# A decoder trunk on one core: the opening transfers in the order of their use, and the mLSTM output factors worked out with tokens on partitions

## The chip, the cores and the metric

The kernel runs on one core of a Trainium2 chip. The metric is the time of one execution on the device in microseconds (us), the median of the runs shown. The engines are called by their names: TensorE (PE: matmuls and transposes), VectorE (DVE), ScalarE (ACT), GpSimd (POOL) and SyncE (SP), which issues most of the transfers.

## What is computed

A trunk of two layers on 512 tokens of width 1024, in float32. Each layer adds half a gated feed-forward block, a token mixer and another half block to the residual; the first layer's mixer is latent attention, the second's an mLSTM. The part of the mLSTM that the change touches is the end of a head: the quotient of `num` by a bounded `den`, a normalisation over the head's 128 values, a gain and a gate.

```python
def rmsnorm(x, g, eps=RMS_EPS):
    y = xf * lax.rsqrt(jnp.mean(xf * xf, axis=-1, keepdims=True) + eps)
    return (y * g.astype(F32)).astype(x.dtype)
...
        h = num / jnp.maximum(jnp.abs(den), jnp.exp(-m_t))[..., None]
...
    hid = mlstm_chunkwise(q, k, v, i_pre, log_f)
    hid = hid * lax.rsqrt(jnp.mean(hid * hid, axis=-1, keepdims=True) + RMS_EPS)
    hid = hid.reshape(B, S, V) * out_norm.astype(F32) * jax.nn.sigmoid(o.astype(F32))
    return hid.astype(h.dtype) @ w_o
...
        x = x + 0.5 * swiglu(rmsnorm(x, ffn_norm[layer, 0]), ffn_w_gate[layer, 0],
                             ffn_w_up[layer, 0], ffn_w_down[layer, 0])
```

With `a = max(|den|, exp(-m))` and `sq` the sum of the squares of `num`, the factor of a head and token is `(sq / 128 + EPS * a * a) ** -0.5`. The kernel works out this one number for every head and token and multiplies `num`, gain and gate by it.

## The kernel before

The activations lie transposed: channels on partitions, the 512 tokens along the free dimension. Every matmul is made of three, from a high and a low part of each operand (`whi`, `wlo` for weights; the first or second of a pair for activations). ScalarE makes the high part, VectorE the low one (`split_pieces`, L185 and L186). The program is written as one sequence, but a scheduler in the tile framework sets the order in which each engine takes its instructions; each engine then works strictly in its order, so an instruction that waits holds all those behind it.

*The opening.* `begin` runs warm-up matmuls of no use to the result, then loads the residual as eight tiles `x` (128x512, two to an arena tile) and the first two weight tiles in quarters (`raw`, 128x256). Quarter k of the first weight tile belongs to `x[k]`, quarter k of the second to `x[4 + k]`: six matmuls use such a pair. `norm_split` makes the parts of `x`. The constants `cst` hold the identity, masks and ones; `st` (L300) is the matmul of the squares `acc` with the ones, from which VectorE, GpSimd and ScalarE make the factor that the feed-forward block behind it waits for, and `bc` (L325) spreads it. SyncE issues the transfers in one queue.

*The mLSTM factors.* In `mlstm`, `mix` adds to one PSUM bank, `rows`, with a selecting weight `pick`: row h gets a head's `den`, row 32 + h its sum of squares, by six matmuls for a pair of heads. `factors` is a generator in three steps, called for heads 0 to 3 and again for 4 to 7. Its steps are put between other work with `defer(n, step)`: the step runs when the n-th weight tile from there is asked for.

- Step one: `a`, `sq` and `n` on 8 partitions x 512 tokens: |den| and a copy on ScalarE, three operations on VectorE. `em` is exp(-m), 8x512.
- Step two: four transposes into `ab` (tokens on partitions, 8 heads and 4 token tiles along the free dimension), the copy `fc` and the power -0.5 on GpSimd, `fp`.
- Step three: four transposes back into `fb`, split into `frows`. `gated` spreads a row over the partitions and multiplies.

In the first call the steps stand among the projections `qk` (the convolution's, `conv(3)`) and `v` (`values(1)`, four weight tiles of 24 matmuls); in the second among the output projections `y`. `columns` transposes other per-head rows into a bank `cb` once and copies them to `cols`.

Of the kernel before, what the change touches and what calls it, by code (L numbers as in the profile page):

```python
# [30 lines left out]
AF = mybir.ActivationFunctionType  # L31
ALU = mybir.AluOpType
AX = mybir.AxisListType

P = 128
# [3 lines left out]
NT = T // P  # L39
# [12 lines left out]
EPS = 1e-6  # L52
# [14 lines left out]
class Trunk:  # L67
# [68 lines left out]
    def load_pieces(self):  # L136

        name, pieces, pool, plus = self.loads[len(self.loaded)]

        ap = self.row(*name)  # L140
        raw = self.duo(pool, F32) if pool else self.wp.tile([P, W], F32, name="raw", tag="raw")
        self.loaded.append(raw)
        for a, b in pieces:
            queue = self.nc.gpsimd if plus and name[0] == "wgs" else self.nc.sync
            queue.dma_start(out=raw[:, a:b], in_=ap[:, a:b])
            yield
        if plus:
            self.nc.gpsimd.dma_start(out=raw, in_=self.row(*plus), accum_op=ALU.add)  # L148
# [185 lines left out]
    def begin(self, gcol):  # L334
        nc = self.nc
        self.used = 0
        self.later = []
        self.mhalf = self.const.tile([P, NT], F32, name="mhalf")
        nc.vector.memset(self.mhalf, -0.5)

        warm = self.small.tile([P, P], BF16, name="warm", tag="warm", bufs=1)
        nc.vector.memset(warm, 0.0)
        nc.scalar.copy(out=warm[:, 0:1], in_=warm[:, 1:2])
        idle = self.ps2.tile([P, T], F32, name="idle", tag="st")
        for i in range(WARM):
            nc.tensor.matmul(idle[:, 0:P], warm, warm, start=True, stop=True)
        self.par = self.const.tile([P, V_END], F32, name="par")
        nc.sync.dma_start(out=self.par, in_=self.t["vecs"])
        cst = self.const.tile([P, self.t["cst"].shape[1]], F32, name="cst")
        self.ident = cst[:, 0:P]  # L350
        self.mask = cst[:, P:2 * P]
        self.maskT = cst[:, 2 * P:3 * P]
        self.invf, self.sign, self.one = (cst[:, 3 * P + i:3 * P + i + 1] for i in range(3))
        self.sel = cst[:, 3 * P + 3:3 * P + 11]
        self.norm_begin(gcol)
        quarters = [(k * 256, k * 256 + 256) for k in range(4)]
        for i in range(2):
            self.loads[i] = self.loads[i][0], quarters, None, None
        for i in range(2):
            load, split = self.load_pieces(), self.split_pieces(quarters, False)  # L360
            for k in range(4):
                d = 4 * i + k
                nc.sync.dma_start(out=self.x[d], in_=self.t["xT"][d * P:(d + 1) * P, :])
                next(load)
                self.norm_split(d)
                next(split)
            list(load), list(split)
            if i == 0:
                nc.sync.dma_start(out=cst, in_=self.t["cst"])
        self.todo = list(range(ND))  # L370

    def constants(self):
# [614 lines left out]
    def mlstm(self, next_gain):  # L987
        nc = self.nc
        v, s = nc.vector, nc.scalar
        xg = self.xg  # L990
        g8 = slice(0, 8)
# [7 lines left out]
        def conv(i):  # L999

            b = self.bank("qk")
            self.project(self.weights("wqk", i), b)
            p, y = self.t512("p"), self.t512("conv")
            v.tensor_tensor(out=p, in0=b, in1=rb, op=ALU.mult)
            v.tensor_scalar(y, p, self.vec(V_CONVW + 3 * ND + i), self.vec(V_CONVB + i), ALU.mult, ALU.add)
            for j in range(1, 4):
                v.scalar_tensor_tensor(out=y[:, j:], in0=p[:, :T - j], scalar=self.vec(V_CONVW + (3 - j) * ND + i),
                                       in1=y[:, j:], op0=ALU.mult, op1=ALU.add)  # L1010
            s.activation(y, y, AF.Silu)
            pr = self.pair()
            if i < 4:
                qz = self.pair("qz")
                for z, e, o in ((qz[0], A, B), (qz[1], B, A)):
                    nc.gpsimd.memset(z[o].bitcast(F32), 0.0)
                    s.copy(out=z[e], in_=y[e])
                s.copy(out=pr[0][B], in_=y[A])
                s.copy(out=pr[1][A], in_=y[B])
                v.tensor_tensor(out=pr[0][A], in0=y[A], in1=qz[0][A].bitcast(F32), op=ALU.subtract)  # L1020
                v.tensor_tensor(out=pr[1][B], in0=y[B], in1=qz[1][B].bitcast(F32), op=ALU.subtract)
                pr = pr + qz
            else:
                self.halves([(pr[0][A], A), (pr[1][B], B)], [(pr[0][B], A), (pr[1][A], B)], y)
            qk[i] = pr
# [18 lines left out]
        tiles = lambda a: a.rearrange("p (a b) -> p a b", a=NT)  # L1044

        def turn(bank, c, src, row=0):

            n, m = src.shape
            nc.tensor.transpose(out=bank[0:m, c:c + n], in_=src, identity=self.ident[row:row + n, row:row + n])

        def small(name, n=32):
            return self.small.tile([P, n], F32, name=name, tag=name, bufs=1)
# [31 lines left out]
        rows, frows = self.pair()  # L1084
        em = self.small.tile([P, T], F32, name="em", tag="rb", bufs=2)
# [24 lines left out]
        values(0)  # L1110
        place = [(0, 0), (1, 0), (2, 0), (1, 384)]
        ws, sums, nums, ys, sg, sg_of, acc, which = {}, {}, {}, {}, {}, {}, {}, {}
        cols = small("cols", 80)

        def columns():

            cb = self.bank("cb")
            for i in range(NT):
                src = z[g8, i * P:(i + 1) * P]
                bt = self.t512("bt") if i < NT - 1 else None  # L1120
                for j in range(i, NT):
                    if j > i:
                        dst = bt[g8, (j - 1) * P:j * P]
                        v.tensor_scalar(dst, src, fl[g8, j * P - 1:j * P], None, ALU.add)
                        src = dst
                    which[i, j] = 8 * len(which)
                    turn(cb, which[i, j], src)
            s.copy(out=cols, in_=cb[:, 0:80])


        def spread(rows, h):
# [83 lines left out]
        def factors(half, squares):  # L1215

            for f in squares:
                f()
            a, n = self.t512("a"), self.t512("n")
            s.activation(a[g8], acc["rows"][g8], AF.Abs)  # L1220
            sq = self.t512("sq")
            s.copy(out=sq[g8], in_=acc["rows"][32:40])
            v.tensor_tensor(out=a[g8], in0=a[g8], in1=em[g8], op=ALU.max)
            v.scalar_tensor_tensor(out=n[g8], in0=a[g8], scalar=EPS, in1=a[g8], op0=ALU.mult, op1=ALU.mult)
            v.scalar_tensor_tensor(out=a[g8], in0=sq[g8], scalar=1.0 / P, in1=n[g8],
                                   op0=ALU.mult, op1=ALU.add)
            yield
            ab = self.bank("ab")
            for j in range(NT):
                turn(ab, 8 * j, a[g8, j * P:(j + 1) * P])  # L1230
            fc, fp = small("fc", 16), small("fp", 16)
            s.copy(out=tiles(fc), in_=tiles(ab[:, 0:32])[:, :, 4 * half:4 * half + 4])
            nc.gpsimd.tensor_tensor(out=fp, in0=fc, in1=self.mhalf[:, 0:1].broadcast_to([P, 16]), op=ALU.pow)
            yield
            fb = self.bank("fb")
            for j in range(NT):
                turn(fb, j * P, fp[:, 4 * j:4 * j + 4])
            self.split_to((frows[0:4], frows[32:36]), fb[0:4])
            yield
# [6 lines left out]
        def out(part, i, between=None):  # L1246
            self.mix_out("wo2", part, i, ys, between)
# [15 lines left out]
        for p in range(3):  # L1263
            a, b = 2 * p, 2 * p + 1
            conv(p + 5) if p < 2 else gate(5)
            gate(a + 2)
            pending = [mix(a), mix(b)]
            if p == 1:
                steps = factors(0, pending)
                for i in (1, 2, 4):  # L1270
                    self.defer(i, lambda: next(steps))
                conv(3)
                values(1)
                for i in range(4):
                    gated(i)
            if p == 0:
                gate(b + 2)
                for f in pending:
                    f()
            if p == 2:  # L1280
                out(0, 0)
            decay(a + 2)
            if p < 2:
                conv((2, 7)[p])
            else:
                for f in pending:
                    f()
            decay(b + 2)
# [203 lines left out]
```

## Time and profile before

| | |
|---|---|
| median of 3 runs | 1839.35 us (1837.66 to 1840.27) |
| the profiled execution | 1836.03 us, span 1834.3 us |
| TensorE busy | 1808.8 us, 99% of the span |
| VectorE, ScalarE, GpSimd busy | 80%, 51%, 10% |
| chain that ended last | TensorE 72%, issue 16%, VectorE 4%, transfers 3%, ScalarE 3%, GpSimd 1% |

A row of the timeline has the start and the duration in us, the engine, the line, the operation, output and inputs, and in brackets the idle time of that engine before it and what ended it. Matmuls overlap in the pipeline: the distance from one start to the next says what one costs, not its duration. The chain is followed back from the last instruction, and busy shares are averages over the whole span.

### The profile page before, as it was taken

Reading aid. Unit: us, or ns where it says so; the run is one execution under the profiler, and the core shown is the slowest. Engines: PE = TensorE matmul, PEld = TensorE weight load, DVE = VectorE, ACT = ScalarE, POOL = GpSimd, SP = SyncE. Lnnn points to the kernel's source line nnn. Section 1 sums busy time; section 2 is a strip of 40 time slices with the busy share of each in tenths; the row PEclk is TensorE's granted clock in tenths of the full one; section 3 lists DMA queues with packets and bytes.
Section 4 is the critical chain, followed back from the end, with each engine's and each line's share of the span. In section 5 each row is a group of like instructions: output and inputs, shape, how many; then the busy total and the mean of one; then the engine's idle time right before and its main releaser. Section 6 shows DMA issues by size and latency. Waiting matters only on the chain.

```text
span 1834.3 us, 30137 instructions
## 1 busy us (share of the span) xinstructions
PE 1808.8 (99%) x12258; PEld 1662.9 (91%) x12258; DVE 1458.8 (80%) x1934; ACT 938.6 (51%) x1350; POOL 181.3 (10%) x233
## 2 busy tenths in 40 slices
PE   9999999999999999999999999999999999999997
PEld 7999989978887999989989999997877779999897
DVE  7887898777767887877797879778878778788875
ACT  5544535567543444534544444455767544445344
POOL 1210001000001210000021000100010012100011
PEclk9999999999999999999999999999999999999999
DMA  8875376421126865466589356633212268753763
GB/s 273 241 221 152 120 189 150 138 75 64 47 94 196 234 190 149 137 184 152 196 217 265 105 162 190 167 106 112 81 63 70 74 186 249 202 151 117 188 150 104
DMA packets 80860, 282.45 MB, mean 154 GB/s; under 512 B 9105, under 2 KB 12305, under 8 KB 80721
## 3 DMA queue, kind: packets, MB, share of 16 engines
q1 hardware_dynamic: 52416, 179.06, 28.2%
q0 software_dynamic: 27728, 100.94, 25.4%
q8 instruction: 96, 1.57, 0.3%
q10 hardware_dynamic: 576, 0.52, 0.1%
q14 instruction: 44, 0.35, 0.1%
HBM read 270.01 MB, written 10.49 MB: 153 GB/s over the span
## 4 chain that ended last, share of the span: by engine, by line
PE 72%; issue 16%; DVE 4%; DMA 3%; ACT 3%; POOL 1%; SPq 0%; POOLq 0%; DVEq 0%; ACTq 0%
PE pz L481 4%; PE pw L479 4%; PE pz L479 4%; PE pw L480 4%; PE pz L480 4%; PE pw L481 4%; PE px L479 4%; PE px L480 4%; PE px L481 4%; PE y L217 3%; PE y L218 3%; PE y L219 3%; DMA sum<-in_wds 2%; PE py L479 2%; PE py L480 2%
## 5 line engine op out<-in xcount | busy, mean ns | idle before, releaser
L185 ACT CAST whi<-raw 128x1024 fp32r<-128x1024 f32 (+1 forms) x278 | 284.4, 1024 | 388.9 <-issue 120.7
L186 DVE TENSOR_TENSOR wlo<-raw,whi 128x1024 fp32r<-128x1024 f32 (+1 forms) x278 | 330.3, 1191 | 110.4 <-ACT whi L185 110.2
L185 ACT CAST whi<-sum 128x1024 fp32r<-128x1024 f32 x208 | 217.4, 1048 | 290.9 <-PE pz L480 72.9
L186 DVE TENSOR_TENSOR wlo<-sum,whi 128x1024 fp32r<-128x1024 f32 x208 | 253.1, 1221 | 67.4 <-ACT whi L185 67.2
L173 DVE TENSOR_TENSOR sum<-raw,sum 128x1024 f32<-128x1024 f32 x88 | 107.3, 1219 | 15.3 <-DMA raw<-in_wgs 14.6
L148 POOL DMA_DIRECT2D sum<-in_wgs x72 | 63.4, 880 | 290.1 <-DMA sum<-in_wgs 273.3
L481 PE MATMUL pz<-b5h,wlo 128*128 128x256 f32 x288 | 81.2, 282 | 0.6 <-DVE wlo L186 0.6
L479 PE MATMUL pz<-b5h,whi 128*128 128x256 f32 x288 | 81.3, 282 | 0.0
L479 PE MATMUL px<-b1h,whi 128*128 128x256 f32 x288 | 81.3, 282 | 0.0
L479 PE MATMUL pw<-b7h,whi 128*128 128x256 f32 x288 | 81.3, 282 | 0.0
L479 PE MATMUL px<-b2h,whi 128*128 128x256 f32 x288 | 81.3, 282 | 0.0
L480 PE MATMUL pw<-b4l,whi 128*128 128x256 f32 x288 | 81.3, 282 | 0.0
L480 PE MATMUL py<-b6l,whi 128*128 128x256 f32 x288 | 81.3, 282 | 0.0
L480 PE MATMUL px<-b1l,whi 128*128 128x256 f32 x288 | 81.3, 282 | 0.0
L479 PE MATMUL py<-b6h,whi 128*128 128x256 f32 x288 | 81.3, 282 | 0.0
L479 PE MATMUL pw<-b4h,whi 128*128 128x256 f32 x288 | 81.3, 282 | 0.0
L479 PE MATMUL pz<-b3h,whi 128*128 128x256 f32 x288 | 81.3, 282 | 0.0
L480 PE MATMUL pz<-b3l,whi 128*128 128x256 f32 x288 | 81.3, 282 | 0.0
L480 PE MATMUL pw<-b7l,whi 128*128 128x256 f32 x288 | 81.3, 282 | 0.0
L480 PE MATMUL px<-b2l,whi 128*128 128x256 f32 x288 | 81.3, 282 | 0.0
L480 PE MATMUL pz<-b5l,whi 128*128 128x256 f32 x288 | 81.3, 282 | 0.0
L481 PE MATMUL pz<-b3h,wlo 128*128 128x256 f32 x288 | 81.2, 282 | 0.0
(423 smaller groups left out, 6201.1 us busy)
## 6 DMA issues: line engine op xcount, KB each, us to landing
sum<-in_wgs POOLq DMA_DIRECT2D x144, 512.0 KB, 6.7
raw<-in_wgs SPq DMA_DIRECT2D x108, 512.0 KB, 5.6
sum<-in_wds POOLq DMA_DIRECT2D x48, 512.0 KB, 6.3
raw<-in_wds SPq DMA_DIRECT2D x48, 512.0 KB, 3.3
sum<-in_wds SPq DMA_DIRECT2D x32, 512.0 KB, 4.4
raw<-in_wgc SPq DMA_DIRECT2D x30, 512.0 KB, 3.6
raw<-in_wdn SPq DMA_DIRECT2D x24, 512.0 KB, 3.7
away<-x SPq DMA_DIRECT2D x16, 512.0 KB, 3.8
```

Source lines behind the costliest of these rows:

```text
L148: self.nc.gpsimd.dma_start(out=raw, in_=self.row(*plus), accum_op=ALU.add)
L173: self.nc.vector.tensor_tensor(out=t, in0=a, in1=b, op=ALU.add)
L185: self.nc.scalar.copy(out=hi[:, a:b], in_=raw[:, a:b])
L186: self.nc.vector.tensor_tensor(out=lo[:, a:b], in0=raw[:, a:b], in1=hi[:, a:b].bitcast(F32), op=ALU.subtract)
L217: mm(out, lhs[0], rhs[0], start=start, stop=False)
L218: mm(out, lhs[0], rhs[1], start=False, stop=False)
L219: mm(out, lhs[1], rhs[0], start=False, stop=stop)
L479: mm(out, wh, bh[:, b], start=first and e + k == 0, stop=False, skip_group_check=True)
L480: mm(out, wh, bl[:, b], start=False, stop=False, skip_group_check=True)
L481: mm(out, wl, bh[:, b], start=False, stop=last and e + k == 4, skip_group_check=True)
```

## The change

In the opening the transfers are written as eight pairs of an `x` and a weight quarter, with `cst` behind all of them; four memsets of one column make each `x` tile's first use an instruction of VectorE, behind which its transfers then stand. In the mLSTM, `em` is transposed with the other columns, step one of `factors` only copies the 40 rows to `both`, and the absolute value, the maximum and the sum are made behind the transposes, on 128 partitions x 16. In the first call the steps are deferred to the weight tiles 2, 3 and 5 instead of 1, 2 and 4.

```diff
-            queue = self.nc.gpsimd if plus and name[0] == "wgs" else self.nc.sync
...
+        for a in self.xt:
+            nc.vector.memset(a[:, 0:1], 0.0)
         for i in range(2):
             self.loads[i] = self.loads[i][0], quarters, None, None
-        for i in range(2):
-            load, split = self.load_pieces(), self.split_pieces(quarters, False)
-            for k in range(4):
-                d = 4 * i + k
+            load = self.load_pieces()
+            for d in range(4 * i, 4 * i + 4):
                 nc.sync.dma_start(out=self.x[d], in_=self.t["xT"][d * P:(d + 1) * P, :])
                 next(load)
-                self.norm_split(d)
+            list(load)
+        for i in range(2):
+            split = self.split_pieces(quarters, False)
+            for k in range(4):
+                self.norm_split(4 * i + k)
                 next(split)
-            list(load), list(split)
-            if i == 0:
-                nc.sync.dma_start(out=cst, in_=self.t["cst"])
+            list(split)
+        nc.sync.dma_start(out=cst, in_=self.t["cst"])
...
-        cols = small("cols", 80)
+        cols = small("cols", 112)
...
-            s.copy(out=cols, in_=cb[:, 0:80])
+            for j in range(NT):
+                turn(cb, 80 + 8 * j, em[g8, j * P:(j + 1) * P])
+            s.copy(out=cols, in_=cb[:, 0:112])
...
-            a, n = self.t512("a"), self.t512("n")
-            s.activation(a[g8], acc["rows"][g8], AF.Abs)
-            sq = self.t512("sq")
-            s.copy(out=sq[g8], in_=acc["rows"][32:40])
-            v.tensor_tensor(out=a[g8], in0=a[g8], in1=em[g8], op=ALU.max)
-            v.scalar_tensor_tensor(out=n[g8], in0=a[g8], scalar=EPS, in1=a[g8], op0=ALU.mult, op1=ALU.mult)
-            v.scalar_tensor_tensor(out=a[g8], in0=sq[g8], scalar=1.0 / P, in1=n[g8],
-                                   op0=ALU.mult, op1=ALU.add)
+            both = self.t512("both")
+            s.copy(out=both[0:40], in_=acc["rows"][0:40])
             yield
             ab = self.bank("ab")
             for j in range(NT):
-                turn(ab, 8 * j, a[g8, j * P:(j + 1) * P])
-            fc, fp = small("fc", 16), small("fp", 16)
-            s.copy(out=tiles(fc), in_=tiles(ab[:, 0:32])[:, :, 4 * half:4 * half + 4])
+                turn(ab, 40 * j, both[0:40, j * P:(j + 1) * P])
+            of = lambda t, c: tiles(t)[:, :, c + 4 * half:c + 4 * half + 4]
+            ab = ab[:, 0:160]
+            fa, fc, fp = small("fa", 16), small("fc", 16), small("fp", 16)
+            s.activation(tiles(fa), of(ab, 0), AF.Abs)
+            v.tensor_tensor(out=tiles(fa), in0=tiles(fa), in1=of(cols[:, 80:112], 0), op=ALU.max)
+            v.scalar_tensor_tensor(out=fa, in0=fa, scalar=EPS, in1=fa, op0=ALU.mult, op1=ALU.mult)
+            v.scalar_tensor_tensor(out=tiles(fc), in0=of(ab, 32), scalar=1.0 / P, in1=tiles(fa),
+                                   op0=ALU.mult, op1=ALU.add)
...
-                for i in (1, 2, 4):
+                for i in (2, 3, 5):
                     self.defer(i, lambda: next(steps))
```

The scheduler's order changes with it. On SyncE, at the start of the program, the rows before are these; `x_78` to `x_81` are the four arena tiles of the residual (two transfers each), `raw_129` and `raw_161` the first two weight tiles, `raw_194` the third.

```order
L348 DMA par_124<-in_vecs 128x111
L363 DMA x_78<-in_xT 128x512
L145 DMA raw_129<-in_wgc 128x256
L363 DMA x_78<-in_xT 128x512
L145 DMA raw_129<-in_wgc 128x256 x3
L369 DMA cst_126<-in_cst 128x395
L363 DMA x_79<-in_xT 128x512 x2
L145 DMA raw_161<-in_wgc 128x256 x4
L145 DMA raw_194<-in_wgc 128x1024
L363 DMA x_80<-in_xT 128x512 x2
L145 DMA raw_200<-in_wgc 128x1024
L363 DMA x_81<-in_xT 128x512 x2
```

Of the change, on SyncE at the same place (here `raw_133` and `raw_142` are the first two weight tiles, `raw_198` the third):

```order
L347 DMA par_124<-in_vecs 128x111
L363 DMA x_78<-in_xT 128x512
L144 DMA raw_133<-in_wgc 128x256
...
L363 DMA x_79<-in_xT 128x512
...
L363 DMA x_80<-in_xT 128x512
L144 DMA raw_142<-in_wgc 128x256
...
L363 DMA x_81<-in_xT 128x512
...
L372 DMA cst_126<-in_cst 128x395
L144 DMA raw_198<-in_wgc 128x1024
L144 DMA raw_204<-in_wgc 128x1024
```

Behind each `x` stands now one quarter of weights, and `cst` and the third weight tile have moved behind the last pair. On TensorE, in the first call of `factors`, the rows before are:

```order
L223 MATMUL rows<-pr,pick 128x512
L219 MATMUL qk<-pr,wlo 128x512
L217 MATMUL qk<-pr,whi 128x512
L218 MATMUL qk<-pr,whi 128x512
L219 MATMUL qk<-pr,wlo 128x512
L1049 MATMUL ab<-cst,a 128x8 x4
L217 MATMUL v<-whi,pr 128x512
```

Of the change, on TensorE at the same place, with the 24 `v` matmuls of the first weight tile cut:

```order
L217 MATMUL qk<-pr,whi 128x512
L218 MATMUL qk<-pr,wlo 128x512
L222 MATMUL rows<-pr,pick 128x512 x4
L216 MATMUL v<-whi,pr 128x512
...
L218 MATMUL v<-whi,pr 128x512
L1052 MATMUL ab<-cst,both 128x40 x4
L216 MATMUL v<-whi,pr 128x512
```

Four of the six `rows` matmuls have moved from among the `qk` matmuls to behind them, and `ab` from ahead of `v` to behind the first 24 of `v`; `fb` has moved by one weight tile as well. On VectorE, in the second call, before:

```order
L1310 TENSOR_TENSOR x<-y,x 128x512
L1223 TENSOR_TENSOR a<-a,em 8x512
L1224 SCALAR_TENSOR_TENSOR n<-a 8x512
L1310 TENSOR_TENSOR x<-y,x 128x512
L1225 SCALAR_TENSOR_TENSOR a<-sq,n 8x512
L186 TENSOR_TENSOR wlo<-raw,whi 128x1024
L1310 TENSOR_TENSOR x<-y,x 128x512 x2
```

Of the change, on VectorE at the same place:

```order
L1315 TENSOR_TENSOR x<-y,x 128x512 x2
L185 TENSOR_TENSOR wlo<-raw,whi 128x1024
L1234 TENSOR_TENSOR fa<-fa,cols 128x16
L1235 SCALAR_TENSOR_TENSOR fa<-fa 128x16
L1236 SCALAR_TENSOR_TENSOR fc<-ab,fa 128x16
L1315 TENSOR_TENSOR x<-y,x 128x512 x2
```

The three operations of 8x512 ahead of `wlo` are gone, and three of 128x16 stand behind it. On TensorE nothing moves in the second call.

## Rows read from the trace of the kernel before

**Rows 1.** Waits of TensorE, whole span: us in total, times, longest.

```profile
PE ab L1049 <- DVE a L1225: 3.9, 2, 2.4
```

**Rows 2.** Timeline of TensorE around `ab` in the first call.

```profile
1355.35 0.40 PE L219 MATMUL qk<-pr,wlo 128*128 128x512 f32 x1
1358.12 0.41 PE L1049 MATMUL ab<-cst,a 8*128 8x8 f32 x4 [2.37 <-DVE a L1225]
...
1359.03 0.60 PE L219 MATMUL v<-whi,pr 128*128 128x512 f32 x1
...
1362.67 0.39 PE L219 MATMUL v<-whi,pr 128*128 128x512 f32 x1
...
1371.09 0.39 PE L219 MATMUL v<-whi,pr 128*128 128x512 f32 x1
```

**Rows 3.** Windows behind both `ab`: busy us by engine, granted clock, DMA share, GB/s.

```profile
1359.00:1362.70 3.70, 3.70 (x11) 2.84 (x10) 2.81 (x4) 1.67 (x2) 3.70 (x1) 0.54 0.38 142
1440.80:1444.50 3.70, 3.70 (x11) 2.86 (x10) 0.14 (x1) 0.00 (x0) 2.44 (x1) 0.54 0.43 142
```

**Rows 4.** Timeline of all engines around `ab` in the second call.

```profile
1436.12 0.59 ACT L1220 ACTIVATE a<-rows 8x512 f32<-8x512 f32 x1 [2.30 <-PE rows L223]
...
1437.57 0.39 PE L219 MATMUL y<-pr,wlo 128*128 128x512 f32 x1
1437.77 1.04 ACT L185 CAST whi<-raw 128x1024 fp32r<-128x1024 f32 x1 [0.46 <-PE y L218]
...
1438.67 0.67 DVE L1225 SCALAR_TENSOR_TENSOR a<-sq,n 8x512 f32<-8x512 f32 x1
1439.27 1.21 DVE L186 TENSOR_TENSOR wlo<-raw,whi 128x1024 fp32r<-128x1024 f32 x1
...
1439.48 0.38 PE L1049 MATMUL ab<-cst,a 8*128 8x8 f32 x4 [1.52 <-DVE a L1225]
...
1440.21 3.03 POOL L1233 TENSOR_TENSOR fp<-fc,mhalf 128x16 f32<-128x16 f32 x1 [77.13 <-ACT fc L1232]
```

**Rows 5.** Timeline of TensorE behind `ab` in the second call.

```profile
1440.83 0.51 PE L218 MATMUL y<-pr,whi 128*128 128x512 f32 x1
...
1444.47 0.40 PE L218 MATMUL y<-pr,whi 128*128 128x512 f32 x1
```

**Rows 6.** Timeline of all engines in the opening (SPq issues transfers).

```profile
4.49 0.91 SPq L363 DMA_DIRECT2D x<-in_xT  x2
4.68 0.39 ACT L185 CAST whi<-raw 128x256 fp32r<-128x256 f32 x1
...
6.07 0.78 PE L217 MATMUL g<-pr,whi 128*128 128x512 f32 x1
...
7.44 0.39 PE L217 MATMUL u<-pr,whi 128*128 128x512 f32 x1
...
9.84 0.72 ACT L232 ACTIVATE pr<-x,par 128x512 fp32r<-128x512 f32 x1 [0.54 <-DMA x<-in_xT]
...
10.62 0.50 PE L217 MATMUL g<-pr,whi 128*128 128x512 f32 x1 [0.92 <-ACT pr L232]
...
14.44 0.50 PE L217 MATMUL g<-pr,whi 128*128 128x512 f32 x1 [0.43 <-ACT whi L185]
...
23.21 0.95 PE L300 MATMUL st<-cst,acc 128*128 128x1 f32 x8
```

**Rows 7.** Timeline of TensorE at `bc` in the opening.

```profile
27.55 0.47 PE L325 MATMUL bc<-diag,onesr 128*128 128x512 f32 x1 [0.24 <-DVE diag L321]
```

**Rows 8.** Instructions of tile zp: ns min/median/max, first and last start, forms.

```profile
L1078 DVE SCALAR_TENSOR_TENSOR zp<-zp,zu x5: 193/193/193, 1266.3 to 1267.2; 128x32 f32<-128x32 f32 x5
```

**Rows 9.** Timeline of GpSimd, the power in the first call.

```profile
1358.88 4.20 POOL L1233 TENSOR_TENSOR fp<-fc,mhalf 128x16 f32<-128x16 f32 x1 [25.45 <-ACT fc L1232]
```

**Rows 10.** Timeline of TensorE, transposes in `columns`.

```profile
1285.35 0.32 PE L1049 MATMUL cb<-cst,bt 8*128 8x8 f32 x3
```

**Rows 11.** The page's slices of 45.9 us: GB/s moved.

```profile
GB/s 273 241 221 152 120 189 150 138 75 64 47 94 196 234 190 149 137 184 152 196 217 265 105 162 190 167 106 112 81 63 70 74 186 249 202 151 117 188 150 104
```

More of the change, by code (lines that the diff above doesn't have):

```diff
@@ L138, in load_pieces @@
         name, pieces, pool, plus = self.loads[len(self.loaded)]
+        queue = self.nc.gpsimd if plus and name[0] == "wgs" else self.nc.sync
         ap = self.row(*name)
```

## The prediction

> **What bounds the kernel now.** TensorE: it is busy for nearly the whole span, so I first asked the view of its waits for the places where it stands still, and then read each place in the timeline. The reader is to see one name at the top of the waits: `ab` waiting for `a`, 3.9 us in two waits, the longest 2.4 [rows 1]. These are the two calls of `factors`. No other cause stands together like that at a place which the diff touches, except the opening.
>
> In the first call the last `qk` matmul starts at 1355.35 and `ab` at 1358.12 [rows 2]. A step between matmuls of 512 columns is (1371.09 - 1362.67) / 36 = 0.234 us there (36 steps lie between these two rows), so `ab` could have started at 1355.58 and the stop cost 2.54 us. Behind the stop there is a second price: from 1359.03 to 1362.67 nine steps take 3.64 us where nine at 0.234 take 2.10, and the granted clock of that stretch is 0.54 instead of 1.00, most of it at the lower of the two levels (1.2 instead of 2.4 GHz) [rows 2, 3]. That is 1.54 us more. The second call shows the same pair: from 1437.57 plus one step, 1437.80, to 1439.48 is 1.68 us of stop [rows 4], and from 1440.83 to 1444.47 nine steps take 3.64 us again at a granted clock of 0.54, 1.54 us more [rows 3, 5]. Together 2.54 + 1.54 + 1.68 + 1.54 = **7.30 us**.
>
> In the opening TensorE runs its warm-up matmuls until the first real one at 6.07, and reaches `st` at 23.21 with 61 matmuls between (the first of them the row at 6.07) [rows 6]. 61 steps of 0.234 end at 20.34, so 2.87 us are lost. The first three steps, 6.07 to 7.44, take 1.37 us instead of 0.70; the 0.67 us between follow the warm-ups whatever the transfers do, and I leave them. The rest, 2.20 us, are holes such as those before 10.62 and 14.44, with ScalarE named as the cause; ScalarE itself had waited for `x` (0.54 us before 9.84) [rows 6]. A hole of 0.24 us before `bc` comes on top [rows 7]. So at most 2.20 + 0.24 = **2.44 us** can be had in the opening.
>
> **The change, part by part.** *Factors, what is taken off the path.* The old chain from `rows` to `ab` is two copies on ScalarE, three VectorE operations on 8x512, 0.67 us for the last, with others queued among them: 1436.12 to 1439.48 in the second call [rows 4]. The new chain has one copy, `both`, in its place. It reads the same bank and as many columns as the old ones, 40 partitions instead of 8, so I take it at the 0.59 us of the nearest row; the bounds are nothing and 1.04 us (the row of `whi`, with twice the columns on 128 partitions) [rows 4]. In the second call `ab` stands where it stood. `both` would start at 1436.12 and end at 1436.71, at 1437.16 by the dear bound, and `ab` is due at 1437.80: no wait by either. In the first call the four last `rows` matmuls move behind all of `qk`, and `ab` behind the 24 matmuls of the first `v` chunk, 5.6 us later, which covers `both` by far. What `ab` waited for is thus gone in both calls, and with the stop the slow clock behind it: 7.30 us.
>
> *What is late next.* Behind `ab` come now `fa` on ScalarE, three VectorE operations on 128x16, the power on GpSimd, and `fb` on TensorE. Operations of 128x32 on VectorE take 0.193 us each, five in a row [rows 8]; 16 columns lie between nothing and that, and I take 0.22 us from one start to the next, 0.7 us for three. In the first call `fb` has moved too, two chunks of `v` (48 matmuls, 11.2 us) behind `ab`; the longest power here took 4.20 us [rows 9], so some 5 us are spare. In the second call `fb` stays 24 `y` matmuls behind `ab`: 1437.80 + 0.31 for `ab` + 24 x 0.234 = 1443.7. The chain there: `whi` holds ScalarE from 1437.77 for 1.04 us [rows 4], `fa` follows to 1438.95; VectorE has `wlo` (1.21 us [rows 4], from 1438.8 when `whi` is done) ahead of the three, so they end at about 1440.7; the power begins at 1440.75. With its 3.03 us [rows 4] it ends at 1443.8, a wait of 0.1 to 0.2 us; with the 4.20 us of the first call [rows 9] at 1444.95, a wait of 1.3 us. I take 0.2: in the second call VectorE has only `x<-y` during the power, as in the row of 3.03, where the call with 4.20 had `wlo` and three `conv` operations beside it.
>
> On this the Trainium skill has a rule ("SBUF — State Buffer", Who interferes with whom): a VectorE instruction with two SBUF inputs contends with a GpSimd instruction that reads SBUF, one with at most one SBUF input does not. `x<-y` has one input in PSUM, so by the rule the power keeps its short time and the wait is the 0.2 us of the sum; by the longer row alone it would be 1.3. The two rows, 3.03 and 4.20 us [rows 4, 9], agree with it.
>
> *What is added.* Four more transposes in `columns`: three of that kind took 0.32 us in all [rows 10], so four lie between 0.2 and 0.43 us; 0.25. They need `em`, made long before. `ab` moves 40 columns instead of 8, eight times in all: between nothing and 0.1 us; 0.1. The wider `cols` copy stands on ScalarE beside `og` matmuls of 5.6 us. So the factors give 7.30 - 0.25 - 0.1 - 0.2 = **6.75 us**; with both dear bounds 7.30 - 0.43 - 0.1 - 1.3, and 1.54 more if the wait at `fb` brings the slow clock, **3.9 us**.
>
> *Opening.* `x` now alternates with quarters of weights, and `cst` and the third weight tile come behind all of them. The third `x` had been issued at 4.49, behind three more transfers at 0.46 us each, and was used at 9.84 [rows 6]; three places earlier makes 8.5. TensorE wants it at the 13th matmul, 7.44 + 9 x 0.234 = 9.55, and ScalarE needs 0.72 us for it: in time. The eighth pair wants 55 + 8 x 384 KB = 3.1 MB landed; at the 273 GB/s of the first slice [rows 11] that is 11.5 us from about 2.3, 13.8; wanted at 7.44 + 39 x 0.234 = 16.6, with 1.5 us of work between: in time by about 1 us. Tightest is the third weight tile, due at the 49th matmul, 7.44 + 45 x 0.234 = 18.0: ScalarE has the last pair (0.72 and 0.39 us), three squares and four copies of `cst` ahead of it, by my estimate 3.3 us from 14, then 1.04 for the tile, 18.4. I put 0.45 us on that. The four memsets hold the first `x` for at most 0.2 us, hidden while the warm-ups run: `whi` was done at 5.07, one us before TensorE took it [rows 6]. So 2.44 - 0.45 = **2.0 us**; bounds 0 (the bytes set the pace and every hole comes back) and 2.44. Later work moves along: `st` stands after 50 matmuls instead of 61, so VectorE, which feeds the stage behind, starts it some 4 us earlier.
>
> Sum: 6.75 + 2.0 = 8.75 us. The profiled execution took 1836.03 us (span 1834.3) and would take 1827.3; the median of the runs shown is 1839.35, so the forecast is **1830.6 us**.
>
> **Rivals.** *Bytes, not order:* in the opening ScalarE waits for `x` as before, because eight transfers in flight share one rate; the 5.35 us from issue to use (4.49 to 9.84) [rows 6] speak for it, the 13.8 worked out for the last pair against. The opening gives 0: 1839.35 - 6.75 = 1832.6. *The power comes late:* 4.20 us in the second call, with the slow clock behind it; the row of 4.20 speaks for it, `x<-y` alone beside it against. 1839.35 - 3.9 - 2.0 = 1833.4. *Handed back later:* the 8.75 us are lost again where TensorE meets a transfer or VectorE that did not move along: about 1839. Against it: the view of the waits names no transfer for TensorE, and loads start when buffers come free, which moves with TensorE. *Slower:* `st` stands now eleven matmuls sooner, ahead of work that could run, and needs all eight squares and `cst`, which is the last transfer of the opening. TensorE takes in order, so if `cst` or the last `x` is late, everything waits. It decides against the change by 0.2% only from 6.75 + 3.7 = 10.4 us of loss over the old opening, `st` near 31 us (33.6 less eleven steps); the bytes put `cst` near 15. The time would be 1843.
>
> **How the numbers follow.** Both parts work: 0.62, 1830.6. Bytes: 0.16, 1832.6. Late power: 0.12, 1833.4. Handed back: 0.07. Slower: 0.03. About 0.2% (3.7 us) is what a measurement here can tell from no change; the first three lie beyond it, so faster 0.90, same 0.07, slower 0.03. The range takes in the first three with the upper bounds of both gains (7.3 + 2.44, 1829.6) and 1.5 us for the spread of a median (1837.66 to 1840.27): 1828.3 to 1835.0.
>
> **What would show it.** Right: no wait of TensorE before either `ab`, steps of 0.234 us and a granted clock of 1.00 for the 10 us behind; `st` between 18.4 and 19.4; `fb` of the second call within 0.3 us of the matmul before it. Wrong: a wait at `fb` or at the `spread` behind it above 1 us; holes before `g` or `st` in the opening that add to 2 us; a wait of TensorE beyond the mLSTM part that is longer than before.

## The result, and the profile after

The changed kernel takes 1815.46 us (median of 4 runs, 1809.45 to 1816.38) where the kernel before takes 1838.51 (4 runs, 1837.06 to 1840.27): a ratio of 0.9867, 95% interval 0.9844 to 0.9891. The forecast was 1830.6 and its range ended at 1828.3. The kernel gained 23 us and not 8.75.

The profiled execution took 1816.38 us, 19.65 less than that of before. The page's first part (engine, busy us, share of the span, instructions) shows TensorE busy for 98% of the span, where it was 99%:

```profile
PE 1785.4 (98%) x12262; PEld 1636.9 (90%) x12262; DVE 1453.5 (80%) x1938; ACT 937.7 (52%) x1348; POOL 180.4 (10%) x233
```

The waits of TensorE after the change (us in total, times, longest) answer to [rows 1]:

```profile
PE bc L324 <- DVE diag L320: 3.8, 7, 1.8
PE py L484 <- DVE wlo L185: 2.8, 3, 1.6
PE idle L345 <- ACT warm L342: 2.3, 1, 2.3
PE dv L626 <- DVE wlo L185: 2.1, 3, 0.8
PE dw L626 <- DVE wlo L185: 1.8, 4, 0.5
PE pz L484 <- DVE wlo L185: 1.6, 4, 0.5
PE dv L624 <- ACT whi L184: 1.3, 1, 1.3
```

`ab` is gone from the list. In its place stand `py`, `dv`, `dw` and `pz`, the quarter products of the FFNs, waiting for split weights: 9.6 us in these five rows. Before, waits of these products for `wlo` came to 1.5 us.

The timeline of after, at the places of [rows 2, 4, 5, 6, 7] and in the FFNs (line numbers are lower by one in the first part of the file, higher by three from `seven` on):

```profile
6.06 0.78 PE L216 MATMUL g<-pr,whi 128*128 128x512 f32 x1
...
18.27 0.50 PE L216 MATMUL g<-pr,whi 128*128 128x512 f32 x1 [0.19 <-ACT whi L184]
...
19.06 1.05 PE L299 MATMUL st<-cst,acc 128*128 128x1 f32 x8
...
24.61 0.47 PE L324 MATMUL bc<-diag,onesr 128*128 128x512 f32 x1 [0.68 <-DVE diag L320]
...
54.55 0.28 PE L482 MATMUL px<-b1h,whi 128*128 128x256 f32 x1
...
113.60 0.28 PE L482 MATMUL px<-b1h,whi 128*128 128x256 f32 x1
...
133.20 0.28 PE L482 MATMUL px<-b1h,whi 128*128 128x256 f32 x1
...
655.93 1.23 DVE L172 TENSOR_TENSOR sum<-raw,sum 128x1024 f32<-128x1024 f32 x1 [4.64 <-DMA raw<-in_wgs]
...
658.94 0.39 PE L484 MATMUL py<-b6h,wlo 128*128 128x256 f32 x1 [1.62 <-DVE wlo L185]
...
1274.74 0.22 PE L1052 MATMUL cb<-cst,z 8*128 8x8 f32 x1
...
1350.73 0.40 PE L218 MATMUL v<-whi,pr 128*128 128x512 f32 x1
1351.06 0.44 PE L1052 MATMUL ab<-cst,both 40*128 40x40 f32 x4
...
1352.56 2.90 POOL L1238 TENSOR_TENSOR fp<-fc,mhalf 128x16 f32<-128x16 f32 x1 [29.18 <-DVE fc L1236]
1352.68 1.23 DVE L185 TENSOR_TENSOR wlo<-raw,whi 128x1024 fp32r<-128x1024 f32 x1 [0.27 <-ACT whi L184]
...
1423.18 0.40 PE L218 MATMUL y<-pr,wlo 128*128 128x512 f32 x1
1423.51 0.44 PE L1052 MATMUL ab<-cst,both 40*128 40x40 f32 x4
...
1426.37 2.89 POOL L1238 TENSOR_TENSOR fp<-fc,mhalf 128x16 f32<-128x16 f32 x1 [70.91 <-DVE fc L1236]
...
1429.34 0.39 PE L218 MATMUL y<-pr,wlo 128*128 128x512 f32 x1
1429.57 0.60 PE L1052 MATMUL fb<-cst,fp 128*4 128x128 f32 x4
...
1505.66 0.28 PE L482 MATMUL px<-b1h,whi 128*128 128x256 f32 x1
```

The same marks in the kernel before:

```profile
55.69 0.28 PE L479 MATMUL px<-b1h,whi 128*128 128x256 f32 x1
...
116.17 0.28 PE L479 MATMUL px<-b1h,whi 128*128 128x256 f32 x1
...
136.33 0.28 PE L479 MATMUL px<-b1h,whi 128*128 128x256 f32 x1
...
659.76 1.23 DVE L173 TENSOR_TENSOR sum<-raw,sum 128x1024 f32<-128x1024 f32 x1 [2.06 <-DMA raw<-in_wgs]
...
1285.26 0.22 PE L1049 MATMUL cb<-cst,z 8*128 8x8 f32 x1
...
1523.13 0.28 PE L479 MATMUL px<-b1h,whi 128*128 128x256 f32 x1
```

Three things are to be read from the two. From the first row to the first `px`, the opening gives 55.69 - 54.55 = 1.1 us. From `cb` to the next `px`, the mLSTM part, 237.87 us became 230.92: 6.95 us. And an FFN unit of 168 matmuls of 256 columns, from one `px` to the next, took 20.16 us before (0.1200 a step) and takes 19.60 now (0.1167). Nothing in the diff touches these matmuls, and there are over 8,700 of them. Steps of 512 columns are 0.233 in both.

Taken over the whole timeline, there are 8,860 steps between two matmuls of 256 columns in either profile. Those up to 0.14 us have a mean of 0.11997 before (8,836) and of 0.11705 after (8,804); the rest, holes, add up to 7.4 us before (24) and 23.5 after (56). So the faster step gives 8,804 x 0.00292 = 25.7 us, and the holes take back 23.5 - 7.4 less the 32 ordinary steps that they replace (3.8), 12.3. With the two predicted parts: 1.1 + 6.95 + 25.7 - 12.3 = 21.5 of the 19.65 that are to be explained; 1.9 us lost elsewhere were not followed.

The windows behind both `ab` (busy us by engine, granted clock, DMA share, GB/s) answer to [rows 3]; the clock is at 1.00:

```profile
1351.00:1355.00 4.00, 4.00 (x20) 3.25 (x20) 2.81 (x6) 3.41 (x6) 2.44 (x1) 1.00 0.02 8
1424.00:1428.00 4.00, 4.00 (x18) 3.23 (x19) 2.66 (x6) 0.50 (x2) 1.63 (x1) 1.00 0.31 96
```

### The profile page after: what moved, and what is told of

Read it like the earlier page. It is cut to its first block, busy times and chain, and to the rows that moved or that the text cites. A ratio compares the mean times of both kernels' runs of the same rounds, so it can differ in the third digit from the quotient of the medians.

```text
span 1814.6 us, 30151 instructions
## 1 busy us (share of the span) xinstructions
PE 1785.4 (98%) x12262; PEld 1636.9 (90%) x12262; DVE 1453.5 (80%) x1938; ACT 937.7 (52%) x1348; POOL 180.4 (10%) x233
## 3 DMA queue, kind: packets, MB, share of 16 engines
q8 instruction: 96, 1.57, 0.3%
## 4 chain that ended last, share of the span: by engine, by line
PE 71%; issue 16%; DVE 6%; DMA 3%; ACT 3%; POOL 1%; SPq 0%; POOLq 0%; DVEq 0%; ACTq 0%
PE pz L484 4%; PE pw L482 3%; PE pw L483 3%; PE pw L484 3%; PE pz L482 3%; PE pz L483 3%; PE px L484 3%; PE px L482 3%; PE px L483 3%; PE y L216 3%; PE y L217 3%; PE y L218 3%; DMA sum<-in_wds 2%; DVE wlo L185 2%; PE py L484 2%
## 5 line engine op out<-in xcount | busy, mean ns | idle before, releaser
L172 DVE TENSOR_TENSOR sum<-raw,sum 128x1024 f32<-128x1024 f32 x88 | 107.2, 1218 | 17.2 <-DMA raw<-in_wgs 15.5
L484 PE MATMUL py<-b6h,wlo 128*128 128x256 f32 x288 | 80.8, 281 | 2.8 <-DVE wlo L185 2.8
L484 PE MATMUL px<-b1h,wlo 128*128 128x256 f32 x288 | 80.5, 279 | 0.0
L484 PE MATMUL pw<-b7h,wlo 128*128 128x256 f32 x288 | 80.5, 279 | 0.0
L484 PE MATMUL px<-b2h,wlo 128*128 128x256 f32 x288 | 80.5, 279 | 0.0
L484 PE MATMUL pw<-b4h,wlo 128*128 128x256 f32 x288 | 80.5, 279 | 0.0
```

What stands on the lines that cost most here:

```text
L172: self.nc.vector.tensor_tensor(out=t, in0=a, in1=b, op=ALU.add)
L484: mm(out, wl, bh[:, b], start=False, stop=last and e + k == 4, skip_group_check=True)
```

## The experiments

The change has a side effect that its words don't tell: `cols` grew by 128 bytes a partition and `fa` came new with 64, both in the pool `small`. The pool `arena` lies behind it in SBUF, so its buffers, which hold the moving operands, moved from address 83648 to 83840, while the split weights `whi` and `wlo`, the stationary ones, stayed (the first at 32608). Buffers of both kinds are 4096 bytes apart. From the first `whi` to the first arena buffer it is 51040 bytes before and 51232 after; what is left of such a number when it is divided by 128 or 256 is called the distance below: 96 before, 32 after, by either.

**Which part does it.** The change was taken apart, and the address moved alone. The first two kernels hold only the diff's part in `load_pieces` and `begin`, or only the rest. The third is the kernel before with this edit, and the fourth the changed kernel with the same one, from 112 to 128:

```
-        cols = small("cols", 80)
+        cols = small("cols", 128)
...
-            s.copy(out=cols, in_=cb[:, 0:80])
+            s.copy(out=cols[:, 0:80], in_=cb[:, 0:80])
```

*e1, the opening alone:*

> The opening of the change alone; the factors and the column tile stay as before, so every large SBUF buffer keeps its old address. Theory A (the 256-column matmul step, 0.1200 us before and 0.1167 us after, follows the SBUF address of the large buffers, which the wider column tile and the new tile fa move up by 192 bytes per partition): the step stays 0.1200, an FFN unit of 168 matmuls 20.16 us, and only the opening's gain of 1.2 to 2.0 us is left: 1836.5 to 1837.3. Theory B (the step follows how far TensorE's weight loads run ahead, and the opening sets that for the whole run): step 0.1167, unit 19.60, 1823 to 1825. Theory C (the factors' instructions do it): as A here.

Measured: 1839.7 us, ratio 0.9991 (0.9976 to 1.0006), step 0.1200. Its profile reaches the first `px` at 53.58, 2.1 us sooner than before, but TensorE then waits for `wlo` at `py`, 2.2 us in three waits, where before it did not.

*e2, the factors alone:*

> The factors of the change alone, the opening as before; the large buffers stand 192 bytes higher. Theory A (address): step 0.1167 in most of the run from the first FFN on, 1838.5 - 7.0 (mLSTM) - about 12 = 1817 to 1821. Theory B (the opening sets it): step 0.1200, only the mLSTM part's gain, 1838.5 - 6.75 = 1831.8. Theory C (the factors' instructions, late in the program): 0.1200 up to 1330 us and 0.1167 only behind.

Measured: 1819.61 us, ratio 0.9893 (0.9875 to 0.9911), mean step 0.1169 from the first FFN on.

*e3, the shift alone:*

> The kernel before, with nothing changed but the size of the tile cols, 128 columns instead of 80 (nothing reads or writes the added ones): every instruction and its order as before, the large buffers 192 bytes per partition higher, as in the changed kernel. Theory A (address): step 0.1167, unit 19.60 us, time 1838.5 - 11 to 14 = 1825 to 1828. Theories B and C: 1838.5, step 0.1200.

Measured: 1822.33 us, ratio 0.9911 (0.9892 to 0.9929), mean step 0.1168. Its FFN unit takes 19.60 us:

```profile
94.41 0.28 PE L479 MATMUL px<-b1h,whi 128*128 128x256 f32 x1
...
114.01 0.28 PE L479 MATMUL px<-b1h,whi 128*128 128x256 f32 x1
```

*e4, the changed kernel 64 bytes on:*

> The changed kernel with nothing changed but the size of cols, 128 columns instead of 112: the large buffers stand 64 bytes higher than in the changed kernel, at an address that leaves 64 when divided by 128, as before the change (after: 0). Theory A (address, with a period of 128 bytes): step 0.1200, unit 20.16 us, time 1815.5 + 11 to 14 = 1827 to 1830, which is the forecast on record. With a longer period of the address it could stay at 0.1167. Theories B and C: 1815.5, step 0.1167.

Measured: 1831.78 us, ratio 0.9954 (0.9941 to 0.9967), step 0.1200. So the address alone makes and unmakes the fast step; theories B and C fall. (The times of e1, e3 and e4 lie 1.8 to 2.7 us outside what theory A gave, beside a kernel before of 1840.9 us in these runs; the steps are as it said.) And at the old step the whole change is worth 0.46%, 8.5 us.

**Which address.** Four shifts of the changed kernel, by the size of `cols` (136, 120, 120 and 136 columns) and in the first two also by this edit, which moves the weights by 32 bytes:

```
-        self.maskb = self.const.tile([P, P], BF16, name="maskb")
+        self.maskb = self.const.tile([P, P + 16], BF16, name="maskb")[:, 0:P]
```

*e5, distance 128:*

> The changed kernel with two tiles made larger and nothing else: maskb by 32 bytes and cols by 96, so that the split weights (stationary, 96 over a multiple of 128 before) and the arena (moving, 0 over a multiple of 128) both stand on multiples of 128 bytes. Theory lines (a moving operand of 256 columns, 1024 bytes, touches 8 lines of 128 bytes where it stands on a line's start and 9 elsewhere; the weights don't matter): step 0.1167 as in the changed kernel, ratio to before 0.987, 1813 to 1820. Theory relation (what counts is the distance between moving and stationary address modulo 128, 96 in the kernel before, 32 in the changed one): the distance is 0 here, a step of either kind. If the weights' reads cost too, the mixed stretches of 0.118 fall to 0.1167 and the ratio to 0.985 or less.

Measured: 1823.18 us, ratio 0.9899 (0.9864 to 0.9934), mean step 0.1187.

*e6, distance 64:*

> The changed kernel, split weights on multiples of 128 bytes, arena 64 bytes over one; nothing else. Theory lines: 9 lines, step 0.1200, ratio to before 0.995 as in the run of the changed kernel with the arena at 64 (about 1830). Theory relation (distance 64): a step other than 0.1200 is possible, 0.1167 and 0.987 if only 96 is bad. If the weights set it: 0.1167.

Measured: 1807.84 us, ratio 0.9823 (0.9795 to 0.9850), mean step 0.1173, and steps of 512 columns at 0.229.

*e7, distance 64:*

> The changed kernel, weights as they were (96 over a multiple of 128), arena 32 bytes over one; nothing else. Theory lines: step 0.1200, ratio 0.995, about 1830. Theory half lines (64 bytes count, so that 0 and 64 would differ only through the pairing of reads): a step other than both. Theory relation (distance 64): as in the run with the weights at 0 and the arena at 64.

Measured: 1806.73 us, ratio 0.9822 (0.9787 to 0.9857), mean step 0.1174, 512 columns at 0.229.

*e8, distance 128:*

> The changed kernel, weights as they were, arena 96 bytes over a multiple of 128 like them; nothing else. Theory lines: step 0.1200, ratio 0.995, about 1830. Theory relation (distance 0): the same step as the run with both on multiples of 128.

Measured: 1823.46 us, ratio 0.9907 (0.9879 to 0.9936), mean step 0.1187.

The theory of lines falls: an arena at 32 or 64 over a multiple of 128 gives the fastest kernel so far, and one on a multiple of 128 a middling one. Runs with equal distance agree with each other (e5 and e8; e6 and e7) though both addresses differ, and runs with the arena at the same address do not (e4 at 1831.78 and e6 at 1807.84, weights 32 bytes apart). It is the distance between the two that counts, not either address. (These runs move the arena against all that lies ahead of it, the temporaries too; that the weights are the other end is argued from what TensorE reads here, weights and arena.)

**Without the change, the period, and one weight tile of the two.** The first kernel is the kernel before with `cols` at 136 columns, the second the changed one with 152. The last two have `cols` at 120 and 128, and a gap of 32 (96) bytes between `whi` and `wlo`:

```
         hi = self.wp.tile([P, W], F32R, name="whi", tag="whi")
+        if not self.split:
+            self.wp.tile([P, 8], F32, name="gap", tag="gap", bufs=1)
         lo = self.wp.tile([P, W], F32R, name="wlo", tag="wlo")
```

*e9, the kernel before at distance 64:*

> The kernel before with cols made 224 bytes larger and nothing else: every instruction and its order as before, the distance from split weights to arena 64 bytes modulo 128 instead of 96. Theory relation (the step follows this distance alone: 64 is the fastest of the four): 1840.9 - (1831.8 - 1807.3), the difference that the changed kernel shows between 96 and 64, = 1816 on the chip of the last calls, a ratio of 0.987 with none of the change in it. Rival (the fast steps of 64 need the change's own order): 1822 or more, as the same kernel showed with 32.

Measured: 1815.62 us, ratio 0.9871 (0.9854 to 0.9889), mean step 0.1171. The kernel before, with one tile made larger, is as fast as the changed kernel. That 64 is faster than 32 is not the 256-column step, which is the same (0.1171 for 0.1168 in e3), but the 512-column one: some 2,680 steps at 0.229 to 0.230 instead of 0.233, 8 to 10 us.

*e10, distance 192:*

> The changed kernel with the arena 128 bytes higher than in the run with distance 64 (weights as they were): the distance is 192, which leaves 64 modulo 128 but not modulo 256. If the period is 128 bytes: 1804 to 1811, ratio 0.982, steps 0.1167 to 0.1178 and 0.229. If it is 256 bytes or more: some other level, 0.987 to 0.995.

Measured: 1799.94 us, ratio 0.9787 (0.9768 to 0.9807), mean step 0.1146, 512 columns at 0.233. The period is not 128, and the kernel is faster than either expectation. It is the fastest of the study, 15.5 us below the changed one. Units in it, early and late:

```profile
94.27 0.28 PE L482 MATMUL px<-b1h,whi 128*128 128x256 f32 x1
...
114.06 0.28 PE L482 MATMUL px<-b1h,whi 128*128 128x256 f32 x1
...
133.49 0.28 PE L482 MATMUL px<-b1h,whi 128*128 128x256 f32 x1
...
949.62 0.28 PE L482 MATMUL px<-b1h,whi 128*128 128x256 f32 x1
...
968.66 0.28 PE L482 MATMUL px<-b1h,whi 128*128 128x256 f32 x1
```

The first unit takes 19.79 us for 168 matmuls, the one at 949.62 takes 19.04, and that at 114.06, 19.43, is a mix. So the mean step of 0.1146 is not one step but two, 0.1178 and 0.1133, in different stretches.

*e11, whi at 96 and wlo at 64:*

> The changed kernel with a gap of 32 bytes between the buffers of whi and wlo, the arena at 64 modulo 128: the distance is 96 (slow) for whi and 64 (fast) for wlo. Each chunk of the contraction has three matmuls: whi with the high part, whi with the low part, wlo with the high part. Theory relation, by loads beside the matmul (a matmul's stream meets the weight load of the next one): slow steps behind the first and the third of the three, since whi is loaded there, two of three, time 1831.8 - 24.5/3 = 1823.6. Theory relation by a matmul's own weights: slow behind the first and the second, the same time. Rival (the address of one of the two alone, or of something that moved along): all steps alike, 1807 or 1832.

Measured: 1817.41 us, ratio 0.9879 (0.9857 to 0.9902). The mean steps behind the first, second and third matmul of a chunk (the three that use one 128x128 block of split weights) are 0.1183, 0.1180 and 0.1170: no clear pattern, and a sum of three below what two steps of 0.1200 and one of 0.1173 would give (0.3533 for 0.3573). A miss.

*e12, whi at 192 and wlo at 96 (by 128: 64 and 96):*

> The mirror of the run before: a gap of 96 bytes, distance 64 (fast) for whi and 96 (slow) for wlo. By loads beside the matmul: one step in three slow, behind the second of the three (wlo is loaded there). By a matmul's own weights: behind the third. Either way about 1807.3 + 24.5/3 = 1815.5. Rival as in the run before: 1807 or 1832.

Measured: 1813.93 us, ratio 0.9866 (0.9843 to 0.9888). Mean steps over some 2,000 chunks each: 0.1145, 0.1233, 0.1156. The slow one is behind the second matmul (L485), as the timeline shows, 0.13 where the others have 0.11 (PEld is the load of weights):

```profile
56.24 0.28 PE L484 MATMUL px<-b1h,whi 128*128 128x256 f32 x1
56.24 0.19 PEld L485 LDWEIGHTS px<-b1l,whi 128*128 128x128 f32 x1
56.35 0.28 PE L485 MATMUL px<-b1l,whi 128*128 128x256 f32 x1
56.36 0.19 PEld L486 LDWEIGHTS px<-b1h,wlo 128*128 128x128 f32 x1
56.48 0.28 PE L486 MATMUL px<-b1h,wlo 128*128 128x256 f32 x1
...
56.59 0.28 PE L484 MATMUL py<-b6h,whi 128*128 128x256 f32 x1
```

While L485 streams (from 56.35), the `wlo` of the next matmul is loaded (from 56.36). So here the slow step stands where the load and the stream that run side by side are 96 apart, not where a matmul is so from its own weights.

Two things weaken this run. It is not the mirror of e11: from `whi` at 32608 to the arena at 84000 it is 192 modulo 256, the distance of e10, and 64 only modulo 128. And the three matmuls of a chunk together take 0.3534 us, which is a unit of 19.79 us. In e6, with both tiles at 64, a unit takes as long, 19.78 by these rounded rows:

```profile
112.85 0.28 PE L482 MATMUL px<-b1h,whi 128*128 128x256 f32 x1
...
132.63 0.28 PE L482 MATMUL px<-b1h,whi 128*128 128x256 f32 x1
```

So e12 shows where the time falls within a chunk, not that a load at 96 made the chunk longer than e6's. That its time came out near the 1815.5 of the expectation is luck, since that sum put one step in three at the level of 96 and two at that of 64.

**The other distances.** The changed kernel with `cols` at 184, 144, 160 and 168 columns:

*e13, distance 320:*

> The changed kernel with the arena moved so that it stands 320 bytes (modulo 512) from the split weights, nothing else: 64 modulo 256. Period 256: as the runs with distance 64, ratio 0.982, 256-column step 0.1178, 512-column step 0.229. Period 512 or longer: another level.

Measured: 1809.76 us, ratio 0.9837 (0.9822 to 0.9852), mean step 0.1172, 512 columns at 0.229: as at 64.

*e14, distance 160:*

> The changed kernel at distance 160 (32 modulo 128). Period 128: as the changed kernel itself (32), ratio 0.987, 0.1167 and 0.2333. Period 256: another level; by the pair 64 and 192, the second half of the period would be a little faster, 0.983.

Measured: 1824.12 us, ratio 0.9915 (0.9893 to 0.9936), mean step 0.1179, 512 columns at 0.234: slower than the 0.983 expected for another level.

*e15, distance 224:*

> The changed kernel at distance 224 (96 modulo 128). Period 128: as the run with distance 96, ratio 0.995, step 0.1200. Period 256: another level, between 0.98 and 0.995.

Measured: 1823.58 us, ratio 0.9912 (0.9897 to 0.9927), mean step 0.1183.

*e16, distance 256:*

> The changed kernel at distance 256 (0 modulo 256). Period 128: as the two runs with distance 128, ratio 0.990, steps 0.1187 and 0.2325. Period 256: another level; if both streams on the same residue are the worst case, slower than at 96, above 0.995.

Measured: 1820.54 us, ratio 0.9897 (0.9880 to 0.9913): steps of 256 columns at 0.1200, as slow as at 96, and of 512 at 0.227, the fastest. The expectation of a ratio above 0.995 is missed by the 512-column steps, some 2,680, which take 17 us less than in e4. Its FFN unit takes 20.16 us, as in the kernel before:

```profile
114.55 0.28 PE L482 MATMUL px<-b1h,whi 128*128 128x256 f32 x1
...
134.71 0.28 PE L482 MATMUL px<-b1h,whi 128*128 128x256 f32 x1
```

320 (e13) has the steps of 64. The kernel before and e1 stand at 352 when divided by 512, e4 at 96, and all three have the step 0.1200. So a period of 256 bytes fits all runs; 128 does not, most clearly by the 512-column steps (0.229 at 64, 0.233 at 192; 0.232 at 128, 0.227 at 256).

## Why the prediction was wrong

**The two predicted parts were right together.** At equal distance the change is worth 0.46% at 96 (e4 over before), 0.44% at 32 (0.9867 over 0.9911, e3) and 0.50% at 64 (0.9822 over 0.9871, e9): 8.1 to 9.2 us, where the sum said 8.75. The interval of e4 alone runs from 0.33% to 0.59%, 6.1 to 10.9 us.

*Factors, 6.75 us:* 6.95 between `cb` and `px`, the sum without its 0.2 us for a wait at `fb`, which did not come. No wait before either `ab` (0.33 us behind the matmul before it, both times), clock 1.00 behind them instead of 0.54. `fb` of the second call stands 0.23 us behind the matmul before it; the power took 2.89 us, so the late power did not come. By the Trainium skill ("SBUF — State Buffer", Who interferes with whom) the power was to keep its short time beside `x<-y`; the trace agrees for this call. The first call does not bear out the rule's other half: its power took 2.90 us from 1352.56, and `wlo`, with both inputs in SBUF, ran beside it from 1352.68 at its usual 1.23 us. The prediction also misread the row of 3.03: `wlo` ran until 1439.27 + 1.21 = 1440.48 there, into a power that began at 1440.21, so that row was not `x<-y` alone.

Part of the 6.95 is not sure to come. In e1, with the old factors, TensorE stood idle for the same 2.37 us before the first `ab`, yet the clock stayed at 1.00 behind it:

```profile
1358.81 0.41 PE L1052 MATMUL ab<-cst,a 8*128 8x8 f32 x4 [2.37 <-DVE a L1228]
...
1359.40:1363.20 3.80, 3.80 (x17) 3.06 (x17) 3.11 (x4) 1.90 (x3) 3.63 (x1) 1.00 0.39 138
```

Its stretch from `cb` to `px` took 236.39 us, and that of e4, at the same step, 231.01: 5.4 us. So the slow clock, 1.54 us each time in the prediction's sum, does not follow every such stop. In medians the factors alone give less still, 2.7 us from e3 to e2, both at 32; four runs each, spread over 4 us, don't settle it.

*Opening, 2.0 us:* 1.1 in this profile and 2.1 in that of the opening alone. `st` came at 19.06, inside the 18.4 to 19.4 given, and the third weight tile was late as forecast: 0.59 from the matmul before it instead of 0.234, 0.36 us for the 0.45. Up to `st`, 1.30 us are lost instead of 2.87 (50 steps of 0.234 from 6.06 end at 17.76), a gain of 1.57. What the sum had wrong is `bc`: it counted its 0.24 us as gained, and `bc` waits 0.68, which takes 0.44 back. One pair of profiles is a rough measure here: of those at 32 and 96, the three with the old opening reach `px` at 54.95 to 56.39, the three with the new one at 53.58 to 54.61. In the medians of the opening alone 1.2 us are left, with an interval that includes nothing.

**The step that failed** is the sum itself: "6.75 + 2.0 = 8.75". It has no term for code that the diff does not touch; I took the 0.12 us step of the FFNs as given. The diff showed `small("cols", 112)` and the new `fa`, but I costed them as instructions and not as bytes that move every buffer behind them. This term is the largest of all: -25.7 us by the faster step, +12.3 for what was handed back. Shown for it: the shift alone gives 18.6 us in medians (e3; 13 to 20 by its interval), and undoing it in the changed kernel gives 1831.78, 1.2 us from the forecast. (A slip beside it: 1829.6 and 1833.4 with 1.5 us on either side make 1828.1 to 1834.9, not 1828.3 to 1835.0; it changes nothing.)

**"Handed back later"** was given 0.07 as a whole and came true in part. My ground, that the waits name no transfer for TensorE, was too narrow: they name VectorE's `wlo`, and VectorE waits for a transfer. The `sum` at 655.93 waited 4.64 us for `raw`, 2.06 before, and TensorE stood 1.62 us at `py` behind it. `sum` starts 3.8 us sooner than before (655.93 for 659.76), while TensorE was 5.3 us ahead at the first `px` of this FFN (594.80 for 600.11): the transfer did not follow, and what TensorE had gained beyond it is lost there. The distance-192 kernel shows the same further on: its ordinary 256-column steps are 0.0025 us shorter than the changed kernel's (8,775 of them, 21.6 us), its holes add up to 33.2 us instead of 23.5, and 15.5 us remain.

**Still open:** why the distance matters. The place of the slow step in e12 fits a collision between the load of the next weights and the stream of moving columns, but e11 did not show it, the chunk of e12 takes no longer than one of e6, and no run takes one of the two streams away. The two are also the only runs in which `whi` and `wlo` are not a multiple of 256 bytes apart, which may itself set the pattern. That is not tested. The Trainium skill says that TensorE reads weights through a second, independent port ("SBUF — State Buffer", A bandwidth-pool intuition that's wrong) and that the spacing of matmuls is set by load and matmul both ("TensorE: Matmul & The Clock Gate", Back-to-back issue gap). The runs agree with the second, in so far as the step depends on where the two operands stand to each other. No run here tests the first; the addresses, at any rate, are not free to choose (mean steps of 0.1146 to 0.1200 us).

## What to carry to other kernels

When a change adds or widens an SBUF tile, list which buffers stand at other addresses afterwards, and time the change against the old code with the same padding: here a padding alone (e9) brought the kernel before to the time of the changed one. Where TensorE is the bound and every matmul loads new weights, try the distance between stationary and moving buffers over one period as a free parameter. And where a rate rises everywhere, look for the transfer that then sets the pace before counting steps times gain.

## What the runs showed of the hardware

In these kernels the step between float32r matmuls that each load 128 columns of weights went with the distance from weight to moving buffers in SBUF, modulo 256 bytes. The 256-column step is the mean over the whole timeline of steps up to 0.14 us, the 512-column step that between 200 and 300 us; the ratio is that of the changed kernel at this distance to the kernel before (which stands at 96).

| distance mod 256 | 256 columns, us | 512 columns, us | ratio |
|---|---|---|---|
| 0 | 0.1200 | 0.227 | 0.9897 |
| 32 (the changed kernel) | 0.1171 | 0.233 | 0.9867 |
| 64 | 0.1172 to 0.1174 | 0.229 | 0.9822, 0.9823, 0.9837 |
| 96 | 0.1200 | 0.233 | 0.9954 |
| 128 | 0.1187 | 0.232 | 0.9899, 0.9907 |
| 160 | 0.1179 | 0.234 | 0.9915 |
| 192 | 0.1146 | 0.233 | 0.9787 |
| 224 | 0.1183 | 0.233 | 0.9912 |

The mean granted clock of the profiled executions is 0.995 to 0.998, so none of this is the clock. Within one kernel the step can also differ from stretch to stretch: in the changed kernel, at distance 32, it is 0.1167 up to 657 us and 0.1178 for a time behind the stop at `py`, with operands at the same distance. The means of 64 and 192 are mixes of the same two levels: a chunk of three takes 0.340 or 0.353 us, the lower in 8 to 16% of the chunks at 64 (e6, e7, e9, e13) and in 73% at 192 (e10). So the table's 256-column means at these two are shares of two levels in one kernel's order, not two fixed steps. What sets the level was not followed.
